# One layer of a hybrid encoder: the last stage's gate weights load through the norm's scratch, and the embeddings' product gets buffers of its own

## The chip, the cores and the metric

The kernel runs on one core of a Trainium2 chip. The metric is the device time of one execution in microseconds (us). The kernel before took 1815.24 us as the median of three runs (1814.98, 1815.24 and 1816.43).

The engines are named as in the profile: PE is TensorE (matrix products; PEld is its weight load), DVE is VectorE, ACT is ScalarE, POOL is GpSimd. SP is the engine whose queue issues nearly all transfers (DMA) of this kernel. Each engine works through its own instructions strictly in the order in which they stand.

## The reference, cut to what matters

The layer handles 1024 prompt tokens and 64 sample tokens of width 1024. The change touches the last two steps of `_layer`, the down projection of the FFN and the per-layer embeddings:

```
    f = (jax.nn.silu(f @ W['w_ffn_gate']) * (f @ W['w_ffn_up'])) @ W['w_ffn_down']
    x = x + _rmsnorm(f, W['norm_ffn_post'])
    gate = jax.nn.sigmoid(_rmsnorm(x, W['norm_ple_pre']) @ W['w_ple_gate'])
    pe = gate * (p @ W['w_ple_proj'])
    x = x + _rmsnorm(pe, W['norm_ple_post'])
```

`w_ffn_down` is 2816 x 1024, `w_ple_gate` is 1024 x 1024. Everything is float32.

## The kernel before

A float32 product is built from two halves: every operand is split into a high part (ACT copies it to the matrix engine's rounded format) and a low part (DVE subtracts), and each product is three matmuls, high by high, high by low and low by high (`split`, lines 124 to 126; `mm3`, line 128). Weights are thus always loaded, split, and then used.

**The down projection** (`ffn_down`) is done in seven block products (i = 0 to 6, the tuple that starts at line 1326), each of 11 steps (p = 0 to 10). A step loads 512 KB: a block of activations from the scratch `sd` and a block of weights from `td` or from `w_ffn_down` itself (`load`, line 1275). ACT and DVE split them, and PE runs 12 matmuls of 512 columns, or 14 in products that also handle the sample tokens against the tile `as` (line 1341). The raw loads rotate through four buffers: two of the tag `wraw` of the pool W, and two `raw` of the pool "ffn2". The split halves rotate through three pairs: two `wh`/`wl` (tags `whi`, `wlo` of W) and one `dh`/`dl`.

**The last stage** works on nine tiles of tokens in the order 4, 5, 6, 7, 0, 8, 1, 2, 3 (`TOKS`). `ple_first` takes a tile's FFN result, normalizes it, adds the residual (`post`), normalizes again, transposes on PE and splits the result into `hT` (`pre`). `ple_second` multiplies `hT` by the split gate weights, takes the sigmoid, multiplies by `q` (the product p @ w_ple_proj, computed at the start of the kernel and kept in the scratch `qd`), normalizes, adds and stores. The first two `ple_first` run inside product 6.

**The gate weights** are eight slabs of 128 x 1024 (512 KB each). `ple_weight` loads one slab, ACT copies its high half into the big tile `H` (free by then), POOL subtracts for the low half. In the kernel before, the slab lies in a `wraw` buffer (`slab`, line 953), and `ple_weight` is called in steps 0 to 8 of product 4: call 0 loads three norm gains, calls 1 to 8 one slab each. `q` lies in a `whi` buffer.

**What sets the order.** The program is recorded in the order of the code; a scheduler then places each engine's instructions by its own estimate of when their inputs and buffers are ready, so a load can stand well ahead of its place in the code. A tile's buffer is reused only after its last reader is done; the waits follow from that.

Of the kernel before, what the change touches and what calls it, by code (L numbers as in the profile page):

```python
# [8 lines left out]
F32 = mybir.dt.float32  # L9
F32R = mybir.dt.float32r  # L10
# [6 lines left out]
D = 1024  # L17
# [51 lines left out]
class Net:  # L69
# [1191 lines left out]
    def ffn_down(self, PA, P):  # L1261

        nc, W = self.nc, self.W
        V, A = nc.vector, nc.scalar
        acc = self.acc = [PA.pool.tile([128, D], F32, name=f"acc{t}") for t in range(9)]
        AS = P.pool.tile([128, 22, 2 * DEC], F32R, name="as")
        sample = self.ad.rearrange("(k p) t -> p k t", p=128)

        def rows(k0, k1):
            s = P.tile([128, 2, 512], F32, "raw", "raw").rearrange("p a b -> p (a b)")[:, :(k1 - k0) * DEC].rearrange("p (k t) -> p k t", t=DEC)  # L1270
            nc.sync.dma_start(s, sample[:, k0:k1])
            self.split(AS[:, k0:k1, :DEC], AS[:, k0:k1, DEC:], s)
        ni = [0]

        def load(i, q, p):

            n = ni[0] = ni[0] + 1
            raw = W.tile([128, 8, 128], F32, name="raw", tag="wraw", bufs=2).rearrange(
                "p (a c) b -> p a (c b)", a=2) if n % 2 else P.tile([128, 2, 512], F32, "raw", "raw")
            nc.sync.dma_start(raw[:, 0], self.sd[p, i])  # L1280
            if isinstance(q, int):
                nc.sync.dma_start(raw[:, 1], self.td[p, q])
            else:
                r = (2 * p + q[0]) * 128
                nc.sync.dma_start(raw[:, 1], self.I["w_ffn_down"][0, r:r + 128, q[1] * 512:q[1] * 512 + 512])
            if n % 3:
                h, l = (W.tile([128, 8, 128], F32R, name=x, tag=t, bufs=2).rearrange("p (a c) b -> p a (c b)", a=2)
                        for x, t in (("wh", "whi"), ("wl", "wlo")))
            else:
                h, l = (P.tile([128, 2, 512], F32R, x, x) for x in ("dh", "dl"))  # L1290
            self.split(h, l, raw)
            return h, l
        lo, hi = slice(0, 512), slice(512, 1024)

        def c11(i, x):
            V.tensor_add(acc[i][:, lo], acc[i][:, lo], x)

        def c21(i, x):
            V.tensor_add(acc[4 + i][:, lo], acc[4 + i][:, lo], x)

        def c22(i, x):
            V.tensor_add(acc[4 + i][:, hi], acc[4 + i][:, hi], x)

        def copy(d, s):
            def f(i, x):
                A.activation(acc[d + i][:, s], x, AF.Copy)
            return f

        def q1(x):
            A.activation(acc[8][:, lo], x, AF.Copy)  # L1310

        def q2(x):
            A.activation(acc[8][:, hi], x, AF.Copy)
            V.tensor_add(acc[8][:, lo], acc[8][:, lo], x)

        def q3(x):
            V.tensor_add(acc[8][:, hi], acc[8][:, hi], x)
        B = {}

        def bank(n):  # L1320
            return self.ps.tile([128, 512], F32, name="z", tag=(XB + ZB)[n])
        self.ps.alias = {}
        rows(0, 16)
        first = []

        for i, q, b, new, end, sq in ((0, (1, 0), 4, True, copy(0, lo), (2, 1, True, q1)),
                                      (1, (0, 0), 0, True, c11, (4, 0, True, q2)),
                                      (2, 3, 0, False, copy(4, lo), None),
                                      (3, 1, 4, True, copy(4, hi), None),
                                      (4, 2, 4, False, c21, None),  # L1330
                                      (5, 0, 0, False, c22, (4, 0, True, None)),
                                      (6, (1, 1), 0, False, copy(0, hi), (4, 1, False, q3))):
            for p in range(11):
                h, l = load(i, q, p)
                if not i and p == 7:
                    rows(16, 22)
                if sq:
                    if sq[2] and not p:
                        Q = bank(sq[0])
                    for j, x in enumerate((h, l)):  # L1340
                        nc.tensor.matmul(Q, AS[:, 2 * p + sq[1]], x[:, 1], start=sq[2] and p == j == 0, stop=p == 10 and j == 1,
                                         skip_group_check=not sq[2])
                    if p == 10 and sq[3]:
                        sq[3](Q)
                for n in range(4):
                    if new and not p:
                        B[b + n] = bank(b + n)
                    c = slice(n * 128, n * 128 + 128)
                    for j, (x, y) in enumerate(((h, h), (h, l), (l, h))):
                        nc.tensor.matmul(B[b + n], x[:, 0, c], y[:, 1], start=new and p == j == 0, stop=p == 10 and j == 2,  # L1350
                                         skip_group_check=not new)
                    if p == 10:
                        end(n, B[b + n])
                if i == 4 and p < 9:
                    self.ple_weight(PA, p)
                if i == 6 and p in (5, 8):
                    self.ps.alias = PAL
                    first.append(self.ple_first(PA, None, len(first)))
        return first

    def ple_weight(self, PA, i):

        nc = self.nc
        if not i:
            self.pw = []
            self.gb = [self.bcast(PA, n) for n in ("norm_ffn_post", "norm_ple_pre", "norm_ple_post")]
            return
        k = i - 1
        raw = self.slab(self.I["w_ple_gate"][0, k * 128:(k + 1) * 128])
        h, l = (self.H[:, k, i, 0:D] for i in range(2))  # L1370
        nc.scalar.activation(h, raw, AF.Copy)
        nc.gpsimd.tensor_sub(l, raw, h)
        self.pw.append((h, l))

    def ple_first(self, PA, P, i):

        nc = self.nc
        gf, gp, _ = self.gb
        t = TOKS[i]
        r, c0 = 128 if t < 8 else DEC, t * 128  # L1380
        x = self.acc[t]
        xr = PA.tile([128, D], F32, "xr", "xr")[:r]
        nc.sync.dma_start(xr, self.x2[c0:c0 + r])
        xs = PA.tile([128, D], F32, "xn", "xn")[:r]
        if t == 8:
            self.low_rows(x[:r], x, xs)
            x = x[:r]
        self.post(PA, [x[:, :512], x[:, 512:]], gf, xr, x, xs)
        PT = P if i % 3 == 2 else PA
        h = PT.tile([128, 8, 256], F32R, "hT", f"hT{i % 3}")  # L1390
        self.pre(PA, x, gp, h[:, :, 0:r], h[:, :, r:2 * r])
        q = self.W.tile([128, 8, 128], F32R, name="wh", tag="whi", bufs=2).bitcast(F32).rearrange("p a b -> p (a b)")[:r]
        nc.sync.dma_start(q, self.qd[c0:c0 + r])
        return x, h, q

    def ple_second(self, P, i, x, h, q):
        nc = self.nc
        U = self.pw
        t = TOKS[i]
        r = x.shape[0]  # L1400
        pe = self.W.tile([128, 8, 128], F32, name="raw", tag="wraw", bufs=2).rearrange("p a b -> p (a b)")[:r]
        xs = P.tile([128, D], F32, "xq", "xq")[:r]
        last = i == 8
        cuts = [slice(a, b) for a, b in (((0, 512), (512, 768), (768, 1024)) if last else ((0, 512), (512, 1024)))]
        for s in cuts:
# [48 lines left out]
def body(tc, I, O, dbg=None, upto=99):  # L1454
    with ExitStack() as ctx:
        N = Net(ctx, tc, I, O, dbg, upto)
        nc = tc.nc
# [80 lines left out]
        with pool("wout", "right") as PW:  # L1538
            N.HS = PW.tile([128, 8, 2 * DEC], F32R, name="HS")
            with pools(tc, "mrgB", dict(braw=1, ga=2, gs=2)) as P:  # L1540
                raw = mA[0].tile([128, TOK], F32, "braw", "braw")
# [10 lines left out]
        PA = ctx.enter_context(pools(tc, "acc", dict(ss=4, xr=1, xn=2, hT0=1, hT1=1)))  # L1552
        with pools(tc, "ffn2", dict(raw=2, dh=1, dl=1), "right") as P:
            A = N.ffn_down(PA, P)
        with pools(tc, "ple", dict(ss=4, hT2=1, xq=1)) as P:
            for t in range(2, 9 + PD):
                if t < 9:
                    A.append(N.ple_first(PA, P, t))
                if t >= PD:
                    N.ple_second(P, t - PD, *A[t - PD])  # L1560
# [27 lines left out]
```

## Time and profile before

| | |
|---|---|
| three runs | 1814.98, 1815.24, 1816.43 us |
| the profiled execution | 1819.19 us, its span 1817.40 us |
| granted TensorE clock, mean over the span | 0.97 of full speed |
| PE / DVE / ACT / POOL busy | 1704.4 / 1040.1 / 728.3 / 524.9 us |
| transfers | 249.83 MB, 137 GB/s mean |
| the down projection's matmuls (line 1350) | 1445.5 to about 1718.5 us of the span |
| the gate weights' eight loads are issued | 1573.7 to 1618.0 us |

The span is the stretch from the first to the last instruction that the trace records; the execution's own time is 1.79 us longer. All durations in this document come from the profiled execution, whose time lies 3.95 us above the runs' median. In rows of a timeline, the first two numbers are start and duration in us; at the end, in square brackets, stands how long the engine was idle before, and what released it.

### The profile page before, as it was taken

How to read it: one execution, taken by the hardware profiler on the slowest of the kernel's cores; microseconds unless marked ns; L12 is line 12 of the kernel's file. 1: busy time of each engine (PE TensorE's matmuls, PEld its weight loads, DVE VectorE, ACT ScalarE, POOL GpSimd, SP SyncE). 2: the span in 40 equal slices, each digit the busy share in tenths (PEclk: the TensorE clock that was granted, in tenths of full speed). 3: DMA queues.
4: the chain of work that ended last, by engine and by line, in shares of the span. 5: the costliest groups of instructions: out<-in, count | busy, mean ns of one | idle time of the engine just before them, and what ended most of it. 6: DMA issues, size and time to landing. Idle time of an engine off the chain costs nothing.

```text
span 1817.4 us, 24624 instructions
## 1 busy us (share of the span) xinstructions
PE 1704.4 (94%) x9092; PEld 1486.6 (82%) x9092; DVE 1040.1 (57%) x1589; ACT 728.3 (40%) x1349; POOL 524.9 (29%) x454
## 2 busy tenths in 40 slices
PE   8999897999999889999999499999999999979998
PEld 6999897988898878798887388888888888858786
DVE  7438725426767777855443865555555444445465
ACT  6431124125555555633322433333333333443443
POOL 2026000012323232233331654444444200031264
PEclk9999898999999998899999799999999999999999
DMA  8352544684443432157333154444444475665232
GB/s 285 96 137 61 119 99 133 219 223 109 103 106 98 94 101 82 45 182 233 124 102 102 42 174 153 146 140 141 147 142 129 142 252 174 196 197 188 91 104 87
DMA packets 209704, 249.83 MB, mean 137 GB/s; under 512 B 25376, under 2 KB 159632, under 8 KB 209568
## 3 DMA queue, kind: packets, MB, share of 16 engines
q1 hardware_dynamic: 208928, 246.81, 45.0%
q0 software_dynamic: 656, 1.44, 0.6%
q8 instruction: 72, 1.18, 0.3%
q14 instruction: 48, 0.39, 0.1%
HBM read 161.13 MB, written 72.32 MB: 128 GB/s over the span
## 4 chain that ended last, share of the span: by engine, by line
PE 74%; DVE 12%; DMA 5%; ACT 3%; issue 2%; POOL 1%; SPq 1%; DVEq 0%; POOLq 0%; ACTq 0%
PE pj L1184 13%; PE tr L1184 7%; PE pj L137 6%; PE pj L139 6%; PE pj L138 6%; PE pj L1350 3%; PE z L1350 3%; DVE p L730 3%; PE z L1184 3%; PE av L806 2%; PE z L138 2%; PE z L139 2%; PE z L137 2%; PE av L1350 2%; PE tr L1350 2%
## 5 line engine op out<-in xcount | busy, mean ns | idle before, releaser
L137 PE MATMUL pj<-H,wh 128*128 128x362 f32 (+3 forms) x648 | 218.0, 337 | 6.1 <-DVE ql L629 3.4
L139 PE MATMUL pj<-H,wl 128*128 128x362 f32 (+3 forms) x648 | 215.2, 333 | 0.6 <-DVE wl L115 0.6
L138 PE MATMUL pj<-H,wh 128*128 128x362 f32 (+3 forms) x648 | 214.8, 332 | 0.0
L126 DVE TENSOR_TENSOR wl<-raw,wh 128x1024 fp32r<-128x1024 f32 x96 | 129.6, 1352 | 122.5 <-ACT wh L125 122.2
L732 POOL TENSOR_TENSOR w<-w,p 128x383 f32<-128x383 f32 (+4 forms) x68 | 92.6, 1371 | 315.3 <-DVE w L734 187.2
L125 ACT ACTIVATE wh<-raw 128x1024 fp32r<-128x1024 f32 x96 | 101.1, 1057 | 124.5 <-PE z L1350 55.9
L137 PEld LDWEIGHTS pj<-H,wh 128*128 128x128 f32 x648 | 123.0, 190 | 7.8 <-DVE ql L629 3.6
L139 PEld LDWEIGHTS pj<-H,wl 128*128 128x128 f32 x648 | 122.7, 189 | 1.5 <-DVE wl L115 0.8
L138 PEld LDWEIGHTS pj<-H,wh 128*128 128x128 f32 x648 | 122.9, 190 | 1.0 <-issue 0.4
L1184 PE MATMUL pj<-H,s 128*128 128x512 f32 x480 | 118.2, 395 | 0.0
L1184 PEld LDWEIGHTS pj<-H,s 128*128 128x128 f32 x480 | 89.8, 188 | 20.8 <-DVE c L1219 0.3
L125 ACT ACTIVATE s<-st 128x512 fp32r<-128x512 f32 x80 | 50.1, 628 | 125.3 <-PE pj L1184 110.9
L126 DVE TENSOR_TENSOR s<-st,s 128x512 fp32r<-128x512 f32 x80 | 66.0, 827 | 46.9 <-ACT s L125 46.0
L148 POOL TENSOR_TENSOR rs<-rs,mhalf 128x1 f32<-128x1 f32 (+1 forms) x54 | 34.7, 644 | 181.8 <-DVE rs L147 181.5
L119 ACT ACTIVATE wh<-raw 128x1024 fp32r<-128x1024 f32 (+1 forms) x52 | 46.6, 898 | 94.8 <-PE av L138 46.3
L781 DVE TENSOR_TENSOR wtl<-tr,wth 128x512 fp32r<-128x512 f32 (+2 forms) x112 | 55.3, 496 | 50.7 <-ACT wth L780 50.3
L780 ACT ACTIVATE wth<-tr 128x512 fp32r<-128x512 f32 (+2 forms) x112 | 50.3, 453 | 84.6 <-PE tr L776 43.9
L115 DVE TENSOR_TENSOR wl<-raw,wh 128x1024 fp32r<-128x1024 f32 (+1 forms) x50 | 51.1, 1021 | 56.5 <-ACT wh L119 56.5
L1120 POOL TENSOR_TENSOR st<-raw 128x512 f32<-128x512 f32 x40 | 57.6, 1442 | 75.9 <-DVE s L126 41.5
L1184 PE MATMUL tr<-T,s 128*128 128x512 f32 x240 | 62.3, 399 | 17.1 <-ACT s L125 17.1
L728 ACT ACTIVATE p<-z 128x512 f32<-128x512 f32 (+4 forms) x116 | 59.0, 509 | 42.7 <-PE z L830 16.7
L730 DVE TENSOR_TENSOR_SCAN p<-p,zero 128x384 f32<-128x384 f32 (+4 forms) x68 | 73.9, 1094 | 0.2
(558 smaller groups left out, 4672.1 us busy)
## 6 DMA issues: line engine op xcount, KB each, us to landing
sd<-c SPq DMA_DIRECT2D x77, 256.0 KB, 2.7
raw<-sd SPq DMA_DIRECT2D x77, 256.0 KB, 2.8
raw<-in_w_in_dram SPq DMA_DIRECT2D x32, 512.0 KB, 5.4
raw<-in_w_ffn_gate_dram SPq DMA_DIRECT2D x22, 512.0 KB, 3.8
raw<-in_w_ffn_up_dram SPq DMA_DIRECT2D x22, 512.0 KB, 4.7
wd<-in_w_ffn_down_dram SPq DMA_DIRECT2D x44, 256.0 KB, 3.5
td<-wd SPq DMA_DIRECT2D x22, 512.0 KB, 3.2
raw<-td SPq DMA_DIRECT2D x44, 256.0 KB, 3.1
```

The source lines that it names most:

```text
L125: self.nc.scalar.activation(wh, raw, AF.Copy)
L126: self.nc.vector.tensor_sub(wl, raw, wh)
L137: self.nc.tensor.matmul(out, wh, xh, start=i == 0, stop=False)
L138: self.nc.tensor.matmul(out, wh, xl, start=False, stop=False)
L139: self.nc.tensor.matmul(out, wl, xh, start=False, stop=i == n - 1)
L728: nc.scalar.activation(p, z, AF.Sigmoid, scale=-1.0)
L730: nc.vector.tensor_tensor_scan(p[:, ::-1], p[:, ::-1], self.zero.to_broadcast([128, n]), 1.0 if carry is None else carry, op0=OP.mult, op1 ...
L732: (nc.gpsimd if e == 'g' else nc.vector).tensor_tensor(w[:, :n - 1], w[:, :n - 1], p[:, 1:], op=OP.mult)
L781: nc.vector.tensor_sub(wl[:, a:b], ps[:, a:b], wh[:, a:b])
L1120: op(t, x, y)
L1184: self.nc.tensor.matmul(out, a[i][:, k], b[j][:, k], start=start and k == i == j == 0, stop=stop and k == 3 and i == 1, skip_group_check=n ...
L1350: nc.tensor.matmul(B[b + n], x[:, 0, c], y[:, 1], start=new and p == j == 0, stop=p == 10 and j == 2, skip_group_check=not new)
```

## The change

`ple_weight` is called at other places, loads into another buffer, and `q` moves to buffers of its own:

```diff
-                if i == 4 and p < 9:
-                    self.ple_weight(PA, p)
+                if (i, p) == (1, 0) or 2 <= i <= 5 and p in (3, 8):
+                    self.ple_weight(PA, 0 if i == 1 else 2 * i - 3 + (p == 8))
...
-        raw = self.slab(self.I["w_ple_gate"][0, k * 128:(k + 1) * 128])
         h, l = (self.H[:, k, i, 0:D] for i in range(2))
+        raw = PA.tile([128, D], F32, "xn", "xn")
+        nc.sync.dma_start(raw, self.I["w_ple_gate"][0, k * 128:(k + 1) * 128])
         nc.scalar.activation(h, raw, AF.Copy)
         nc.gpsimd.tensor_sub(l, raw, h)
...
-        q = self.W.tile([128, 8, 128], F32R, name="wh", tag="whi", bufs=2).bitcast(F32).rearrange("p a b -> p (a b)")[:r]
-        nc.sync.dma_start(q, self.qd[c0:c0 + r])
-        return x, h, q
-
-    def ple_second(self, P, i, x, h, q):
+        return x, h
+
+    def ple_second(self, P, i, x, h):
...
+        q = P.tile([128, D], F32, "q", "q")[:r]
+        nc.sync.dma_start(q, self.qd[t * 128:t * 128 + r])
...
-        with pools(tc, "ple", dict(ss=4, hT2=1, xq=1)) as P:
+        with pools(tc, "ple", dict(ss=4, hT2=1, xq=1, q=2)) as P:
```

So the code has two slabs in each of the products 2 to 5, the slabs lie in the two `xn` buffers (the scratch of the norms, unused until `ple_first`), and `q` is loaded in `ple_second`. In the built program the two `q` buffers begin at bytes 205248 and 209344 of each partition; `as`, the sample tokens of the down projection, lies at 201696 to 212960, so `q` can be loaded only after the last matmul that reads `as`. `xq`, at 201152, lies over `as` before and after.

The scheduler does not keep the slabs where the code has them. SP's queue in product 0, where the norm gains (`gb_...`) are loaded; `ad` holds the sample tokens, `xr` a residual, `sd` and `in_w_ffn_down` a step's operands. Before:

```order
L950 DMA gb_norm_ple_pre<-in_norm_ple_pre_dram 128x1024
L950 DMA gb_norm_ple_post<-in_norm_ple_post_dram 128x1024
L1383 DMA xr<-x_8619 128x1024
L1271 DMA raw<-ad 128x6x64
L1280 DMA raw<-sd 128x512
L1285 DMA raw<-in_w_ffn_down_dram 128x512
```

The same place of SP's queue now:

```order
L950 DMA gb_norm_ple_pre<-in_norm_ple_pre_dram 128x1024
L950 DMA gb_norm_ple_post<-in_norm_ple_post_dram 128x1024
L1371 DMA xn<-in_w_ple_gate_dram 128x1024 x2
L1271 DMA raw<-ad 128x6x64
L1384 DMA xr<-x_8619 128x1024
L1280 DMA raw<-sd 128x512
L1285 DMA raw<-in_w_ffn_down_dram 128x512
```

Two slabs stand ahead of `ad` and of the operands of product 0's steps 10 and 9, which follow in this order, before as now. The third and fourth slab stand four steps' operands further on, the others singly; all eight stand ahead of product 2's first load.

ACT in products 0 and 1, as the difference (`H` is written by the slabs' copies, `wh` and `dh` by the splits of the steps, `as` by that of the sample tokens):

```order
 L125 ACTIVATE dh<-raw 128x1024
 L125 ACTIVATE wh<-raw 128x1024 x2
-L125 ACTIVATE dh<-raw 128x1024
+L1372 ACTIVATE H<-xn 128x1024
+L125 ACTIVATE dh<-raw 128x1024
+L1372 ACTIVATE H<-xn 128x1024
 L125 ACTIVATE as<-raw 128x6x64
 L125 ACTIVATE wh<-raw 128x1024 x2
 L125 ACTIVATE dh<-raw 128x1024
-L125 ACTIVATE wh<-raw 128x1024
+L1372 ACTIVATE H<-xn 128x1024
+L125 ACTIVATE wh<-raw 128x1024
```

The copies of the slabs now stand between the splits of product 0's last steps and product 1's first ones; the eighth stands behind the split of product 1's step 6, and product 4 has none.

ACT at the end of product 6 (`L1306` copies its four sums out, `L1414` is the sigmoid, `xn` and `xq` are norms, `acc_13218` to `acc_13221` the tiles 4 to 7 and `acc_13214` tile 0). Before:

```order
L982 ACTIVATE xn,ss<-acc_13221 128x512 x2
L1414 ACT_TABLE_LOAD
L1414 ACTIVATE raw<-z 128x512
L1010 ACTIVATE xn,ss<-acc_13221 128x1024
L982 ACTIVATE xn,ss<-acc_13214 128x512
L1414 ACTIVATE raw<-z 128x512
L125 ACTIVATE wh<-raw 128x1024 x2
L125 ACTIVATE hT<-tr 128x4x128 x2
L982 ACTIVATE xq,ss<-raw 128x512 x2
L1306 ACTIVATE acc_13214<-pj 128x512
```

The same place now:

```order
L125 ACTIVATE wh<-raw 128x1024 x2
L1010 ACTIVATE xn,ss<-acc_13220 128x1024
L125 ACTIVATE hT<-tr 128x4x128 x2
L982 ACTIVATE xn,ss<-acc_13221 128x512 x2
L1306 ACTIVATE acc_13214<-pj 128x512
L1306 ACTIVATE acc_13215<-pj 128x512
L1306 ACTIVATE acc_13216<-av 128x512
L1306 ACTIVATE acc_13217<-z 128x512
L1010 ACTIVATE xn,ss<-acc_13221 128x1024
```

The last two splits of product 6 stood behind both sigmoids of the first `ple_second`; now they stand ahead of all of them, and the first sigmoid comes after the sums are copied out.

## Rows read from the trace of the kernel before

**Rows 1.** The page's first part: busy us, share of the span, instructions.

```profile
PE 1704.4 (94%) x9092; PEld 1486.6 (82%) x9092; DVE 1040.1 (57%) x1589; ACT 728.3 (40%) x1349; POOL 524.9 (29%) x454
```

**Rows 2.** Table by stretch: length, busy us per engine (instructions), granted clock, DMA share, GB/s.

```profile
core 0: us, PE busy (x) PEld busy (x) DVE busy (x) ACT busy (x) POOL busy (x), PEclk, DMA share, GB/s
1445.00:1490.00 45.00, 45.00 (x197) 36.49 (x196) 23.24 (x24) 18.08 (x21) 0.00 (x0) 1.00 0.80 263
1490.00:1522.00 32.00, 32.00 (x142) 26.23 (x141) 12.95 (x12) 11.08 (x11) 0.00 (x0) 1.00 0.52 165
1522.00:1590.00 68.00, 68.00 (x300) 55.81 (x299) 31.56 (x27) 30.86 (x34) 2.88 (x2) 1.00 0.61 192
1590.00:1630.00 40.00, 28.78 (x108) 21.61 (x107) 15.00 (x9) 15.60 (x16) 17.54 (x7) 0.91 0.63 204
...
1700.00:1720.00 20.00, 16.35 (x68) 12.28 (x66) 6.97 (x10) 8.56 (x17) 1.36 (x3) 0.91 0.10 29
1720.00:1800.00 80.00, 80.00 (x366) 64.50 (x366) 52.67 (x74) 35.92 (x84) 43.23 (x28) 1.00 0.32 108
```

**Rows 3.** Timeline, products 4 and 5: PE's longest waits.

```profile
1593.05 0.51 PE L1350 MATMUL z<-dl,dh 128*128 128x512 f32 x1 [1.40 <-DVE dl L126]
...
1607.35 0.89 PE L1350 MATMUL z<-dh 128*128 128x512 f32 x2 [4.60 <-ACT dh L125]
...
1618.41 1.22 PE L1350 MATMUL z<-wh 128*128 128x512 f32 x2 [3.69 <-ACT wh L125]
```

**Rows 4.** Chain that ended last, 1580 to 1630 us, in order of time.

```profile
1582.65 5.71 DMA raw<-in_w_ple_gate_dram
...
1589.52 2.41 POOL H L1372
...
1592.32 3.13 DMA raw<-td
...
1595.55 1.07 ACT wh L125
```

**Rows 5.** Timeline of the end of product 6: PE's two waits, ACT, DVE.

```profile
1708.77 0.50 PE L1341 MATMUL z<-wh,as 128*128 128x512 f32 x1 [2.50 <-ACT wh L125]
...
1715.09 0.50 PE L1341 MATMUL z<-wh,as 128*128 128x512 f32 x1 [1.15 <-ACT wh L125]
```

```profile
1707.66 1.06 ACT L125 ACTIVATE wh<-raw 128x1024 fp32r<-128x1024 f32 x1 [0.76 <-DVE raw L1415]
```

```profile
1706.94 0.69 DVE L1415 TENSOR_TENSOR raw<-raw,wh 128x512 f32<-128x512 f32 x1 [3.29 <-ACT raw L1414]
```

**Rows 6.** SP's queue in product 0: issue and its length.

```profile
1462.63 0.79 SPq L1383 DMA_DIRECT2D xr<-x  x1
...
1470.34 0.42 SPq L1285 DMA_DIRECT2D raw<-in_w_ffn_down_dram  x1
```

**Rows 7.** Table by stretch, ten us of product 0.

```profile
1460.00:1470.00 10.00, 10.00 (x46) 8.21 (x45) 4.01 (x4) 3.18 (x3) 0.00 (x0) 1.00 0.89 318
```

**Rows 8.** Timeline, product 0's step 9: ACT's split, DVE's, and PE's use of each.

```profile
1475.35 1.06 ACT L125 ACTIVATE wh<-raw 128x1024 fp32r<-128x1024 f32 x1 [2.33 <-DMA raw<-in_w_ffn_down_dram]
```

```profile
1476.44 1.23 DVE L126 TENSOR_TENSOR wl<-raw,wh 128x1024 fp32r<-128x1024 f32 x1 [2.83 <-ACT wh L125]
```

```profile
1480.20 0.40 PE L1341 MATMUL av<-wh,as 128*128 128x512 f32 x1
...
1481.36 0.39 PE L1341 MATMUL av<-wl,as 128*128 128x512 f32 x1
```

**Rows 9.** Timeline: DVE's subtraction without and with POOL's beside it.

```profile
1586.32 1.22 DVE L126 TENSOR_TENSOR wl<-raw,wh 128x1024 fp32r<-128x1024 f32 x1 [3.46 <-ACT wh L125]
...
1590.42 2.58 DVE L126 TENSOR_TENSOR dl<-raw,dh 128x1024 fp32r<-128x1024 f32 x1 [2.87 <-ACT dh L125]
```

**Rows 10.** DMA issues: KB each, median us to landing; 1440 to 1520, then all.

```profile
xr<-x SPq DMA_DIRECT2D x1, 512.0 KB, 9.1
```

```profile
raw<-in_w_ple_gate_dram SPq DMA_DIRECT2D x8, 512.0 KB, 4.1
wh<-qd SPq DMA_DIRECT2D x8, 512.0 KB, 3.5
```

**Rows 11.** Waits, 1570 to 1640: us in total, times, longest.

```profile
ACT H L1371 <- DMA raw<-in_w_ple_gate_dram: 14.9, 8, 3.2
```

## The prediction, made before the changed kernel was run

> **What bounds the kernel now.** I began with the page's busy times: PE is busy for 94% of the span [rows 1], so the kernel gets faster where PE stops waiting, and nowhere else. The second view was the table by stretch over the part that the change can reach, the down projection and the last stage [rows 2]. The reader is to look for stretches whose PE time is shorter than the stretch. There are two. From 1590 to 1630 PE is busy 28.78 of 40 us, and its granted clock is 0.91, so part of what it does runs at 1.2 in place of 2.4 GHz. From 1700 to 1720 it is busy 16.35 of 20 us, again at 0.91. In the four other stretches shown PE has no gap and the full clock.
>
> The third view was the timeline of the first gap, for what PE waits on: splits of its own steps, by ACT or DVE, the longest 4.60 and 3.69 us [rows 3]. The chain of waits says why these are late [rows 4]: a slab of gate weights takes 5.71 us to land, POOL subtracts for 2.41 us, and only then is the step's operand loaded (3.13 us) and split (1.07 us). The slab lies in one of the four raw buffers through which the steps' operands run, so each slab takes that buffer out of the rotation until POOL is done. The timeline of the second gap [rows 5] shows ACT's split of product 6's step 9 released by DVE's product with `q`, which reads a `wh` buffer; PE then waits 2.50 and 1.15 us for the two last splits.
>
> **The change part by part.**
>
> *The slabs leave the raw buffers and product 4.* What goes is the first gap. Its idle time is 40 - 28.78 = 11.2 us, and the lost clock (1 - 0.91) x 40 = 3.6 us, together 14.8 [rows 2]. Counted another way: the stretch before it runs 300 matmuls in 68 us, so 40 us should hold 176; there are 108, and the 68 missing at 0.227 us are 15.5. I take 15.0. The low end is 11.2, if the clock did not come back with the idle time; the high end 15.5. Products 4 and 5 would then look like the stretch from 1522 on, which has the same operands and no gap. No other wait stands right behind the one removed: the splits there are released by PE itself.
>
> *The slabs arrive in products 0 and 1.* The same eight loads (512 KB), eight ACT copies of 1.06 us and eight POOL subtractions of 2.4 us are done there, and this is where the change must pay. The cover is that PE's operands are split ahead of use. In product 0's step 9, the tightest that I found, ACT ends at 1476.41 and PE needs the result at 1480.20; DVE ends at 1477.67 and PE needs that at 1481.36 [rows 8]. The slack is 3.8 and 3.7 us. Against it stand:
> - the transfers. From 1460 to 1470 the DMA engines are 0.89 busy and move 318 GB/s [rows 7]. SP's queue is in order and already backed up: the residual issued at 1462.63 lands after 9.1 us [rows 6, 10], and step 9's weights, issued at 1470.34, are what ACT waits for until 1475.35 [rows 6, 8]. Two slabs ahead of them add 2 x 0.524 MB / 318 GB/s = 3.3 us.
> - ACT's copies, which wait for their slab in order, with the splits queued behind them. Of the two copies of 1.06 us, most lies in the 2.33 us in which ACT is idle anyway before that split [rows 8]. I count nothing for these.
> - POOL's subtraction beside DVE's: 2.58 against 1.22 us, 1.36 more [rows 9].
>
> The sum at step 9 is 3.3 + 1.4 - 3.7 = 1.0 us of waiting. The next pair of slabs goes out about 15 us later, at the start of product 1, with the backlog draining (the DMA share falls to 0.52 from 1490 on, rows 2); I put 0.5 us on it and nothing on the four that follow singly. So 1.5 us. The low end is 0. The high end: both pairs at 3.3 + 2.1 + 2.4 (two copies and a whole subtraction in the way) - 3.7 = 4.1 us each, and behind each the clock cost that the second gap shows, (1 - 0.91) x 20 = 1.8 us [rows 2]: 12 us. I take the value near the low end, because the rows that set it are measured in that very stretch.
>
> The Trainium skill, "SBUF — State Buffer", section "Who interferes with whom", speaks against this move: VectorE and GpSimd share a port pair as an exclusive lock, so that one of them waits for the other's whole instruction. This trace agrees: the subtraction of 2.58 us began inside one of POOL's. By that rule a DVE split could lose up to a whole POOL instruction, 2.4 us, in place of my 1.36, and the wait at step 9 would be 2.0 us in place of 1.0.
>
> *`q` leaves the `whi` buffers.* What goes is the second gap: 20 - 16.35 = 3.65 us idle and 0.09 x 20 = 1.8 us of clock, 5.4 together [rows 2]. The last two splits of product 6 no longer wait for the first tile's sigmoid and product, and stand ahead of them on ACT. PE loses nothing by having its filler (the first tile's gate products) moved behind: all of that work remains and is ready, and with tiles 4 to 6 transposed it is 3 x 48 matmuls at 0.227 us, 33 us, while ACT copies the sums out. What is late next is `q` of the first tile, which must wait for the last read of `as` and then 3.5 us for its landing [rows 10]. DVE needs it after the first half of the first gate product and its sigmoid, which is 24 matmuls or 5.4 us after the down projection's end; so it arrives earlier than it is needed. The low end is 0, if a new wait takes the place of the old one; the high end 5.4. I take 5.4, as the 80 us behind it run without a wait at POOL 43 and DVE 53 us busy [rows 2], and there PE has more work, not less, to cover the others.
>
> The rest (the residual's load behind `ad`, the gains' call in product 1, which the scheduler leaves where it was) moves nothing that PE waits for: 0.
>
> Sum: -15.0 - 5.4 + 1.5 = -18.9 us. Against the profiled execution that is 1819.19 - 18.9 = 1800.3, and against the median of the runs, 3.95 us lower, 1815.24 - 18.9 = 1796.3. I predict on the median's basis.
>
> **The rivals.**
> 1. *The slabs stall products 0 and 1 in earnest.* For it: the DMA share of 0.80 there against 0.63 where they are now [rows 2], and landings of 9.1 us against 4.1 [rows 10]. Against: the slack of 3.7 us, and that slabs no longer hold up the steps' own buffers. At the high end of the cost, 12 us: 1815.24 - 20.4 + 12 = 1806.8; from 5 us on 1799.8. Time 1800 to 1807.
> 2. *The second gap comes back.* `q`'s buffers lie over `as`; were DVE, in order, to stop at the first product with `q`, the splits of the next tile's transposes would queue behind it and PE would run dry. Against: 3.5 us to land against 5.4. The 5.4 us are lost: 1801.7.
> 3. *Slower.* The copies of the slabs hold ACT for every slab, as now: eight slabs cost 15.0 us now, 1.9 each, of which ACT's waits for their landing are 14.9 in all [rows 11]. Where a landing takes 9.1 in place of 4.1 us, and the splits stand behind the copies in order, each slab would cost about twice that, 3.8 us: 30 us in products 0 and 1 against 20.4 gained, 1824.8. It decides for slower from (20.4 + 3.6) / 8 = 3.0 us per slab. Against: it needs slack near zero at every slab, and after 1490 the DMA engines are half idle.
>
> That the slabs are not spread as the code has them, two to a product, is no rival: the order shows it, and the sum is made for where they stand.
>
> **How the numbers follow.** The forecast has 0.77, with 1793 to 1800 as its own range (0 to 4 us of cost, 1 us for the spread of the runs and the sum's first term); rival 1 has 0.11, rival 2 0.08, rival 3 0.04. The predicted time is 1796.3. The range from 1792.5 to 1806 takes in the forecast, rival 2 and most of rival 1; it leaves out rival 3 and the worst of rival 1. A change of 0.2%, 3.6 us, is about what can be told from none here. Faster: all of the forecast and rival 2, and rival 1 but for a rest, 0.93. The same: a rival 1 worse than I bounded it, 0.03. Slower: 0.04.
>
> **What would show it right or wrong.** In the table by stretch, products 4 and 5 with PE busy throughout at clock 1.00. In product 0, PE's wait at step 9 near 1 us, and none over 2 us up to product 2; if several of 3 us stand there, with ACT's copies of the slabs ahead of them, rival 1 or 3 holds. At the end of product 6, no idle PE before the last two steps; a wait of DVE on `q` with PE idle behind it means rival 2. The prediction would be wrong, too, if the gap in products 4 and 5 stayed without any slab in it: then the raw buffers were not its cause.

## The result, and the profile after

The changed kernel takes 1793.57 us (median of 4 runs, 1792.61 to 1796.34) beside 1815.11 us of the kernel before on the same chip (1810.88 to 1816.43): ratio 0.9888, 95% interval 0.9868 to 0.9907. The forecast was 1796.3.

The profiled execution took 1793.02 us, its span 1791.2. That is 26.2 us less span than before, but not all of it is the change's. The first matmul `tr<-wh,wl` of product 0 starts at 1450.30 us before and at 1443.67 now; what runs up to there is not touched by the change. The timelines of PE, before and after:

```profile
1450.30 0.40 PE L1350 MATMUL tr<-wh,wl 128*128 128x512 f32 x1
```

```profile
1443.67 0.40 PE L1350 MATMUL tr<-wh,wl 128*128 128x512 f32 x1
```

So I compare from this matmul to the end of the span ("from product 0 on"): 1817.4 - 1450.3 = 367.1 us before, 1791.2 - 1443.7 = 347.5 after, a gain of 19.6. The table by stretch, cut at equal distances from that matmul: 78 us (products 0 and 1 and the start of 2), 122 us (most of products 2 to 5), 80 us (product 6 and the first tiles), the rest. Columns as in [rows 2]. Before:

```profile
1450.30:1528.30 78.00, 78.00 (x341) 63.66 (x340) 37.11 (x37) 28.98 (x32) 0.00 (x0) 1.00 0.67 221
1528.30:1650.30 122.00, 110.78 (x467) 89.10 (x466) 55.10 (x43) 52.97 (x57) 20.43 (x8) 0.97 0.62 199
1650.30:1730.30 80.00, 76.35 (x339) 61.50 (x338) 39.32 (x55) 34.76 (x61) 21.62 (x17) 0.98 0.37 120
```

After:

```profile
1443.70:1521.70 78.00, 76.43 (x329) 61.04 (x328) 48.41 (x37) 35.44 (x39) 21.14 (x8) 1.00 0.80 269
1521.70:1643.70 122.00, 122.00 (x538) 100.70 (x537) 55.73 (x49) 50.65 (x56) 0.00 (x0) 1.00 0.58 186
1643.70:1723.70 80.00, 80.00 (x372) 65.35 (x371) 55.46 (x76) 44.16 (x88) 37.48 (x27) 1.00 0.38 129
```

Read the number of PE's matmuls in each. In the middle stretch it rises from 467 to 538: 71 more at 122 / 538 = 0.227 us are 16.1 us gained, and the stretch is full. So are the 80 us behind it, in which product 6 ends (its last matmul starts at 1680.26 now). In the first it falls from 341 to 329, 12 x 0.227 = 2.7 us lost: POOL, idle there before, now has its eight subtractions. What is left of the 19.6, 6.2 us, came behind product 5.

Two waits of PE stand in products 0 and 1, both for a low half by DVE, in the second and sixth step of product 1 (p = 1 and p = 5). Here they are, the first with the rows on either side:

```profile
1482.36 0.63 PE L1350 MATMUL pj<-wh 128*128 128x512 f32 x2
1483.91 0.50 PE L1341 MATMUL z<-wl,as 128*128 128x512 f32 x1 [0.92 <-DVE wl L126]
1484.24 0.39 PE L1350 MATMUL pj<-wl,wh 128*128 128x512 f32 x1
...
1498.90 0.50 PE L1341 MATMUL z<-wl,as 128*128 128x512 f32 x1 [0.56 <-DVE wl L126]
```

Undisturbed, a matmul starts every 0.227 us and its row lasts 0.39, so the idle time in brackets is less than the delay. From 1482.36 to 1484.24 three starts take 1.88 us in place of 0.68: the first wait costs 1.2 us. The second costs 0.8 by the same count. Three more delays, too short to be listed as waits, cost 0.8 together; each stands behind a low half that DVE made beside POOL. The sum is 2.8 us, the loss that the matmuls show.

The timelines of DVE, POOL and ACT (of the changed kernel) ahead of the first wait show what delays it:

```profile
1481.26 2.59 DVE L126 TENSOR_TENSOR wl<-raw,wh 128x1024 fp32r<-128x1024 f32 x1 [2.78 <-DMA raw<-in_w_ffn_down_dram]
```

```profile
1480.36 5.75 POOL L1373 TENSOR_TENSOR H<-xn,H 128x1024 fp32r<-128x1024 f32 x2 [8.44 <-ACT H L1372]
```

```profile
1479.22 1.06 ACT L1372 ACTIVATE H<-xn 128x1024 fp32r<-128x1024 f32 x1 [2.00 <-DMA xn<-in_w_ple_gate_dram]
1480.18 1.04 ACT L125 ACTIVATE wh<-raw 128x1024 fp32r<-128x1024 f32 x1
```

ACT waits 2.00 us for the slab, with the step's split behind it. Then POOL starts on the slab 0.9 us before DVE starts on the step, and DVE takes 2.59 in place of 1.22 us [rows 9]. So two things make the low half late: ACT's split comes late, and DVE's subtraction takes longer.

`q` arrives early: its first load is issued at 1677.92 and lands 3.3 us later (median of 8), and DVE's first product with it is at 1687.8.

### The profile page after: what moved, and what is told of

The parts are those of the page before. It is cut to its first block, busy times and chain, and to the rows that moved or that the text cites. A ratio compares the mean times of both kernels' runs of the same rounds, so it can differ in the third digit from the quotient of the medians.

```text
span 1791.2 us, 24621 instructions
## 1 busy us (share of the span) xinstructions
PE 1688.2 (94%) x9092; PEld 1474.8 (82%) x9092; DVE 1049.7 (59%) x1589; ACT 728.4 (41%) x1349; POOL 527.2 (29%) x454
## 4 chain that ended last, share of the span: by engine, by line
PE 73%; DVE 13%; DMA 6%; ACT 3%; issue 3%; SPq 1%; POOL 1%; DVEq 0%; POOLq 0%; ACTq 0%
PE pj L1184 14%; PE tr L1184 8%; PE pj L137 6%; PE pj L139 6%; PE pj L138 6%; DVE p L730 3%; PE z L1350 3%; PE z L1184 3%; PE pj L1350 3%; PE tr L1350 2%; PE z L138 2%; PE z L137 2%; PE z L139 2%; PE av L806 2%; PE tr L776 1%
## 5 line engine op out<-in xcount | busy, mean ns | idle before, releaser
L126 DVE TENSOR_TENSOR wl<-raw,wh 128x1024 fp32r<-128x1024 f32 x96 | 135.7, 1416 | 105.4 <-ACT wh L125 102.4
```

The source lines that it names most:

```text
L126: self.nc.vector.tensor_sub(wl, raw, wh)
```

## The experiments

"From product 0 on" is taken from each kernel's profile, "idle" is the sum of PE's own waits of over 0.15 us in it. Times are medians beside those of the kernel before on the same chip: 1815.11 for the changed kernel, 1814.50 for `q_only`, `weights_only`, `place_only` and `held4`, 1815.57 for `held`, `buffer_only`, `every2` and `q_late`, 1813.25 for `held_early`, `changed_again` and `dve_low`.

| kernel | us | ratio, 95% | from product 0 on | idle |
|---|---|---|---|---|
| before | 1815.11 | | 367.1 | 14.83 |
| `q_only` | 1810.12 | 0.9974 [0.9963, 0.9986] | 361.0 | 10.13 |
| `weights_only` | 1803.26 | 0.9933 [0.9917, 0.9949] | 352.3 | 5.36 |
| `every2` (one run) | 1800.89 | | 353.5 | 4.55 |
| `place_only` | 1797.84 | 0.9902 [0.9885, 0.9919] | 348.6 | 1.42 |
| `held4` | 1797.12 | 0.9903 [0.9886, 0.9920] | 348.6 | 1.62 |
| `held` | 1798.89 | 0.9897 [0.9880, 0.9915] | 349.4 | 2.54 |
| `held_early` | 1794.60 | 0.9903 [0.9887, 0.9920] | 347.7 | 2.24 |
| changed | 1793.57 | 0.9888 [0.9868, 0.9907] | 347.5 | 1.48 |
| `changed_again` | 1795.29 | 0.9897 [0.9883, 0.9912] | 347.4 | 1.45 |
| `buffer_only` | 1798.81 | 0.9905 [0.9886, 0.9923] | 349.8 | 2.49 |
| `q_late` | 1795.85 | 0.9890 [0.9875, 0.9905] | 347.7 | 1.61 |
| `dve_low` | 1793.64 | 0.9888 [0.9873, 0.9903] | 344.8 | 0 |

All diffs are against the changed kernel and shortened at `...`.

**`q_only`**: the gate weights as before.

```diff
-                if (i, p) == (1, 0) or 2 <= i <= 5 and p in (3, 8):
-                    self.ple_weight(PA, 0 if i == 1 else 2 * i - 3 + (p == 8))
+                if i == 4 and p < 9:
+                    self.ple_weight(PA, p)
...
-        raw = PA.tile([128, D], F32, "xn", "xn")
-        nc.sync.dma_start(raw, self.I["w_ple_gate"][0, k * 128:(k + 1) * 128])
+        raw = self.slab(self.I["w_ple_gate"][0, k * 128:(k + 1) * 128])
```

> The gate weights go through the wraw buffers in product 4, as before; only q has its own buffers and is asked for in ple_second. Theory (q, asked for before the last splits, took their wh buffers): the gap at the end of product 6 goes, 5.4 us by the idle time and the clock of rows 2, so 1809.7 us beside 1815.1; in the trace no wait of PE for the splits of product 6's last two steps, while the gap in products 4 and 5 stays, with PE idle 11 us in 40. Rival (the gap in products 4 and 5 leaves the operands late to the end, so that the second gap hangs on the first): the second gap stays and the time is 1815.

Measured: -6.1 us from product 0 on. PE's longest waits are still in products 4 and 5, and none is left behind them:

```profile
1523.70:1645.70 122.00, 111.76 (x467) 89.91 (x466) 55.20 (x43) 53.13 (x57) 19.93 (x8) 0.96 0.61 199
1645.70:1725.70 80.00, 80.00 (x370) 65.77 (x369) 50.79 (x68) 43.51 (x79) 29.29 (x21) 1.00 0.40 131
```

The second gap is `q`'s and doesn't hang on the first.

**`weights_only`**: `q` as before.

```diff
+        q = self.W.tile([128, 8, 128], F32R, name="wh", tag="whi", bufs=2).bitcast(F32).rearrange("p a b -> p (a b)")[:r]
+        nc.sync.dma_start(q, self.qd[c0:c0 + r])
-        return x, h
+        return x, h, q
...
-        q = P.tile([128, D], F32, "q", "q")[:r]
-        nc.sync.dma_start(q, self.qd[t * 128:t * 128 + r])
...
```

> The gate weights go through xn as in the changed kernel; q is asked for in ple_first and lies in a wh buffer, as before. Theory (two independent causes): the gap in products 4 and 5 goes and 1.6 us of waits come in products 0 and 1, the end of product 6 keeps its waits of 2.50 and 1.15 us: -15.0 + 1.6 = -13.4, 1801.7 us beside 1815.1; q alone and weights alone add up to the whole, -21.5, within 3 us. Rival (the second gap hangs on the first): already as fast as the changed kernel, 1793.6.

Measured: -14.8 us from product 0 on. The end of product 6 has its old waits of [rows 5], to the hundredth:

```profile
1694.32 0.50 PE L1341 MATMUL z<-wh,as 128*128 128x512 f32 x1 [2.50 <-ACT wh L125]
1699.06 0.50 PE L1341 MATMUL z<-wh,as 128*128 128x512 f32 x1 [1.15 <-ACT wh L125]
```

By the profiles the parts add up: -6.1 - 14.8 = -20.9 against -19.6 together. By the times they don't within the 3 us that I had allowed: 4.4 and 11.2 us, 15.6 in all, against 21.5 (18.0 in `changed_again` below); the intervals of these ratios are 4 to 7 us wide. What the profiles show is that each gap stays when the other is gone, so neither hangs on the other.

**`place_only`**: the spread calls, but through `wraw`.

```diff
-        raw = PA.tile([128, D], F32, "xn", "xn")
-        nc.sync.dma_start(raw, self.I["w_ple_gate"][0, k * 128:(k + 1) * 128])
+        raw = self.slab(self.I["w_ple_gate"][0, k * 128:(k + 1) * 128])
```

> As the changed kernel, q included, but the gate weights are loaded into the wraw buffers, two to a product in products 2 to 5. Theory (a slab takes one of the four raw buffers out of the steps' rotation until POOL is done, some 8 us from issue to release by rows 4, so the step that takes that buffer next is late): the gap is spread, not gone: some of the eight slabs cost PE a wait of 1 to 2 us each, since a product's other steps can win back part between them; 1798 to 1806 us. Rival (eight slabs in ten steps were too close together for SP's queue, ACT and POOL; the buffer doesn't matter): no waits in products 2 to 5, at most the 1793.6 us of the changed kernel, or 1792 as products 0 and 1 have no slabs.

**`held4`**: `xn`, at the old place: the calls as in `q_only`, and each load behind the step's.

```diff
...
-        nc.sync.dma_start(raw, self.I["w_ple_gate"][0, k * 128:(k + 1) * 128])
+        with self.tc.issue_after(self.ld.ins):
+            nc.sync.dma_start(raw, self.I["w_ple_gate"][0, k * 128:(k + 1) * 128])
```

> As the changed kernel, q included, and the gate weights in xn, but each of their loads is held behind a load of a step of product 4, so that they run in products 4 and 5, where they ran before. Theory (the raw buffers): the same loads, copies and subtractions at the old place cost nothing or little, since the steps' raw buffers stay in rotation: 1792 to 1795 us, no wait of PE over 1 us from 1590 to 1630. Rival (their traffic, copies on ACT and POOL's subtraction beside DVE's, is the cost): the gap of 11 us comes back with the clock's 3.6, 1807 us.

These two cross place and buffer. `held4` has the old traffic at the old place, and most of the gap is gone: 1.62 us of idle PE in place of 10.13 in `q_only`, which differs in the buffer and in that no load is held there. The loads of `held4` are not further apart: the eight are issued within 30.5 us, in `q_only` within 43.7. Of the 71 matmuls that the gap cost the middle stretch, 54 are back (521 against 467). So the buffer was most of the cost; the 17 still missing, 3.9 us, are what the copies, POOL's work and the transfers can have cost at most, and the time, 1797.12, lies 2 us above what I had expected. But `place_only` has the old buffers, and most of the gap is gone there too (1.42 us idle, 16 matmuls missing, 1797.84): my expectation of 1 to 2 us for each of several slabs failed. The middle stretch of `place_only`, then of `held4`:

```profile
1523.50:1645.50 122.00, 120.46 (x522) 97.23 (x521) 62.34 (x48) 55.14 (x61) 16.84 (x7) 1.00 0.65 215
```

```profile
1526.00:1648.00 122.00, 120.38 (x521) 98.57 (x520) 64.61 (x48) 57.15 (x62) 20.25 (x8) 0.99 0.66 216
```

A slab in a raw buffer costs much only where the next follows soon. How soon was the next question.

**`every2`**: through `wraw`, one slab in every second step from product 4 on.

```diff
-                if (i, p) == (1, 0) or 2 <= i <= 5 and p in (3, 8):
-                    self.ple_weight(PA, 0 if i == 1 else 2 * i - 3 + (p == 8))
+                s = i * 11 + p - 44
+                if (i, p) == (1, 0) or 0 <= s < 16 and s % 2 == 0:
+                    self.ple_weight(PA, 0 if i == 1 else s // 2 + 1)
...
+        raw = self.slab(self.I["w_ple_gate"][0, k * 128:(k + 1) * 128])
```

> As the changed kernel, q included, but the gate weights go through wraw, one in every second step from product 4 on (before: one in every step; the spread one: two in eleven). Theory (a slab holds one of the four raw buffers for a time, and how much of it PE sees depends on how many steps the rotation has to recover before the next slab): the gap between the two, 4 to 10 us of idle PE in products 4 and 5, so 352 to 358 us from product 0 on where the spread one takes 348.6 and slabs in every step 361.0. Rival (only slabs in successive steps hurt, as two of them then follow each other in one of the two wraw buffers with a single step between): 348.6 +- 0.5.

Measured: 353.5 us, 4.55 idle, inside the theory's range. With `wraw` and `q` alike, slabs in every step, in every second, and two in eleven leave 10.13, 4.55 and 1.42 us of idle PE. SP's queue and POOL show the hold: a slab's load goes out at 1586.74, POOL ends with it at 1591.41 + 2.39 = 1593.80, and at 1593.83 the next slab's load goes out:

```profile
1586.74 0.33 SPq L956 DMA_DIRECT2D raw<-in_w_ple_gate_dram  x1
1593.83 0.33 SPq L956 DMA_DIRECT2D raw<-in_w_ple_gate_dram  x1
```

```profile
1591.41 2.39 POOL L1373 TENSOR_TENSOR H<-raw,H 128x1024 fp32r<-128x1024 f32 x1 [4.69 <-ACT H L1372]
```

This slab holds its buffer for 7.1 us, and from the third slab on each load goes out within 0.03 us of POOL's end on the one before. In `place_only` the loads are 12.7 to 17.8 us apart.

**`buffer_only`**: the calls as in `q_only`, the rest as changed. On all five engines the instructions stand in the same order as in the changed kernel.

> As the changed kernel, but the gate weights are asked for where the kernel before asks, in product 4, one in each of the first nine steps. The instructions stand in the same order on every engine as in the changed kernel, since their loads move up to where xn is free either way. Theory: the place in the code does nothing once the buffer is xn; 1793.6 us, the part from product 0 on 347.5 +- 0.5. Rival (something else than the order differs, as addresses or semaphores): a difference of over 1 us.

Measured: 1798.81 us, with a ratio whose interval overlaps that of the changed kernel; 349.8 us in its profile, 2.3 more, although the order is the same. By its own sign the expectation failed. One of its two waits was 1.87 us, and in four us right behind it the granted clock was 0.57 and 11 matmuls ran, where 17 or 18 run at full clock, 1.5 us lost:

```profile
1510.00:1514.00 4.00, 4.00 (x11) 3.15 (x11) 2.02 (x2) 0.00 (x0) 0.00 (x0) 0.57 0.62 189
```

The same order took 347.4 and 347.7 us in `changed_again` and `q_late`, so I take the 2.3 us for what two profiles of one order can differ by, which the later comparisons have to allow for; that addresses or semaphores differ is not ruled out by one profile. The place that the code names did not change the order; the buffer decided where the slabs run.

**`q_late`**: `q` in a `wh` buffer, asked for in `ple_second`.

```diff
-        q = P.tile([128, D], F32, "q", "q")[:r]
+        q = self.W.tile([128, 8, 128], F32R, name="wh", tag="whi", bufs=2).bitcast(F32).rearrange("p a b -> p (a b)")[:r]
         nc.sync.dma_start(q, self.qd[t * 128:t * 128 + r])
...
```

> As the changed kernel, but q lies in a wh buffer, as before; it is asked for in ple_second, as in the changed kernel. The instructions stand in the same order on every engine. Theory (what cost PE was that q was asked for ahead of the last two steps' splits, not which buffer it has; asked for behind them it takes a wh buffer that nobody needs): no waits at the end of product 6, the part from product 0 on 347.5 +- 0.5, 1793.6 us. Rival (its own buffers matter, since a wh buffer is given back only when the down projection's last matmul has read it, later than DVE needs q): 1 to 5.4 us slower.

Measured: 1795.85 us, 347.7. `q`'s own buffers were not needed: `weights_only` has the same `wh` buffer and loads `q` in `ple_first`, and takes 352.3. What counted was asking for it behind the last steps' splits.

**`held`** and **`held_early`**: `xn`, and each load held as in `held4`, at the places that the code names (steps 3 and 8 of products 2 to 5), or at steps 0 and 5.

> As the changed kernel, and each load of gate weights held behind the load of the step at which the code calls it, so that they run two to a product in products 2 to 5, in xn. Theory (in products 0 and 1 the backlog of transfers and the subtraction beside POOL's cost 1.6 us; from product 2 on there is slack for one slab at a time): no wait of PE over 0.3 us from product 0 to the end of product 6; the part from product 0's first product of the weights to the end, 347.5 us in the changed kernel, takes 346, and the time is 1792. Rival (wherever a slab's split meets the steps' own it costs about the same, as with the spread slabs in wraw and the held ones in product 4, 1.7 and 1.6 us): 347.5, 1793.5.

> As held, but the gate weights' loads are held behind steps 0 and 5 of products 2 to 5 in place of 3 and 8. Theory (the 2.54 us of the held one came from one slab whose copy stood on ACT ahead of the copies of a product's sums and waited for its landing; moved away from a product's end it finds slack): no wait of PE over 0.3 us in the down projection, 346.0 +- 0.4 us from product 0 on, 1.5 to 3.8 us less than the runs of the changed kernel's order (347.5 and 349.8), as a time about 1792 to 1796. Rival (a slab's copy that waits for its landing on ACT in order costs 1.5 to 2.5 us wherever it is): 347.5 to 349.

Both theories failed: no wait in products 0 and 1, but others elsewhere, 2.54 and 2.24 us. In `held`, ACT stands for 2.57 us before a slab that hasn't landed, with the copies of product 3's sums behind it, and PE waits for these banks. ACT's timeline, and PE's:

```profile
1577.37 1.06 ACT L125 ACTIVATE wh<-raw 128x1024 fp32r<-128x1024 f32 x1 [1.66 <-PE tr L1350]
1581.00 1.06 ACT L1373 ACTIVATE H<-xn 128x1024 fp32r<-128x1024 f32 x1 [2.57 <-DMA xn<-in_w_ple_gate_dram]
1581.96 1.07 ACT L1306 ACTIVATE acc<-z 128x512 f32<-128x512 f32 x2
```

```profile
1582.60 0.50 PE L1350 MATMUL z<-dh 128*128 128x512 f32 x1 [2.54 <-ACT acc L1306]
```

`held_early` avoids that one, and PE waits 0.90 and 1.34 us for low halves by DVE, each time 2.6 us long beside a subtraction on POOL. Its 347.7 us lie in the rival's range, but not by the rival's cause. Here are DVE and POOL at the first:

```profile
1524.11 2.59 DVE L126 TENSOR_TENSOR wl<-raw,wh 128x1024 fp32r<-128x1024 f32 x1 [4.11 <-ACT wh L125]
```

```profile
1523.21 2.42 POOL L1374 TENSOR_TENSOR H<-xn,H 128x1024 fp32r<-128x1024 f32 x1 [14.08 <-ACT H L1373]
```

POOL ends at 1525.63, DVE at 1526.70, 1.07 us later. In `held_early` and in `place_only` each of the eight slabs brings such a pair with it, in `held` five do: ACT copies the slab and then splits the step it had held up, so that POOL begins about one ACT copy before DVE.

**`changed_again`** and **`dve_low`**: the changed kernel once more, and the low halves of the gate weights on DVE.

```diff
-        nc.gpsimd.tensor_sub(l, raw, h)
+        nc.vector.tensor_sub(l, raw, h)
```

> The changed kernel once more, beside held_early on the same chip. Expected by both theories: 1793 to 1799 us; PE waits 1.5 to 2.6 us in all in products 0 and 1, each time for a low half by DVE, 347.5 to 350 us from product 0 on.

> As the changed kernel, but the low halves of the gate weights are subtracted on DVE in place of POOL. Theory (the waits of 0.5 to 1.9 us in products 0 and 1 come from DVE's subtractions of a step beside POOL's, 2.6 to 3.0 in place of 1.2 us): POOL idle there, every subtraction 1.2 us, no wait of PE for a low half over 0.3 us, 346.0 to 346.5 us from product 0 on. Rival (the waits come from transfers that land late or from ACT): the waits of 1.5 us or more stay, and eight more subtractions on DVE make them no shorter.

Measured: with `dve_low` PE has no wait from product 0 to the last stage: 344.8 us, 2.6 less than `changed_again` and below the 346.0 to 346.5 expected. The grouped rows of DVE and POOL over 1440 to 1525 us, of the changed kernel:

```profile
L126 DVE TENSOR_TENSOR wl<-raw,wh 128x1024 fp32r<-128x1024 f32 x17 | 27.3, 1618 | 20.9 <-ACT wh L125 17.9 <-DMA raw<-in_w_ffn_down_dram 2.8
...
L1373 POOL TENSOR_TENSOR H<-xn,H 128x1024 fp32r<-128x1024 f32 x8 | 21.1, 2652 | 60.3 <-ACT H L1372 60.3
```

and of `dve_low`, with the first stretch of its table:

```profile
L126 DVE TENSOR_TENSOR wl<-raw,wh 128x1024 fp32r<-128x1024 f32 x17 | 20.7, 1223 | 20.5 <-ACT wh L125 20.5
L1373 DVE TENSOR_TENSOR H<-xn,H 128x1024 fp32r<-128x1024 f32 x8 | 9.8, 1222 | 5.5 <-ACT H L1372 5.4
```

```profile
1446.20:1524.20 78.00, 78.00 (x341) 63.58 (x340) 46.03 (x45) 36.26 (x40) 0.00 (x0) 1.00 0.80 274
```

The slabs still run in products 0 and 1, with the DMA share as high (0.80 in both), and PE is back at the 341 matmuls of before; the five kernels that have POOL's subtractions there show 319 to 330. But not only POOL is out: the scheduler places the slabs' loads anew, the third of them two steps' operands further ahead, and product 1's second step is split 33.5 us behind product 0's first `tr<-wh,wl`, in the changed kernel 36.5. The timeline of `dve_low` at product 0's step 9, DVE and PE:

```profile
1475.95 1.22 DVE L126 TENSOR_TENSOR wl<-raw,wh 128x1024 fp32r<-128x1024 f32 x1 [3.37 <-ACT wh L125]
```

```profile
1477.23 0.50 PE L1341 MATMUL av<-wl,as 128*128 128x512 f32 x1
```

The low half is ready at 1475.95 + 1.22 = 1477.17, and PE takes it at 1477.23. Of the 3.7 us of slack [rows 8] less than 0.1 is left. So late transfers alone came just short of a wait, and `dve_low` by itself doesn't part them from POOL. The changed kernel does, at its first wait. The kernel before at the same step, DVE's subtraction and the first uses of the high and of the low half by PE:

```profile
1484.73 1.23 DVE L126 TENSOR_TENSOR wl<-raw,wh 128x1024 fp32r<-128x1024 f32 x1 [2.01 <-ACT wh L125]
```

```profile
1488.45 0.40 PE L1341 MATMUL z<-wh,as 128*128 128x512 f32 x1
...
1490.76 0.40 PE L1341 MATMUL z<-wl,as 128*128 128x512 f32 x1
```

Counted from product 0's first `tr<-wh,wl`, DVE is done at 1485.96 - 1450.30 = 35.7 us before and at 1483.85 - 1443.67 = 40.2 in the changed kernel, 4.5 later: 3.2 by ACT's later split, the rest by the longer subtraction. The slack was 1490.76 - 1485.96 = 4.8 us. But PE's order there has changed, too: before, it comes to the low half 2.3 us after the high one, now three matmuls, 0.7 us, after it. That leaves 3.2 us of slack, 3.5 with the 0.3 that PE is late by then. By this count neither the late split nor the pair alone would have made PE wait; together they make 4.5 us, and it waits. The times can't tell the two kernels apart (1793.64 and 1795.29 us on one chip, overlapping intervals); the 2.6 us are read from the profiles alone, one of each.

## Why the prediction was right, and where it was not

**The slabs leave the raw buffers: -15.0 predicted, -16.1 measured** by matmuls in the middle stretch. `held4` against `q_only` shows the buffer as the cause of 54 of the 71 matmuls, 12.3 us. The prediction left out that the cost per slab is no constant: `every2` and `place_only` show that it grows as the slabs follow closer, and that spreading them in the old buffers would have won nearly as much. Rival 3's price of 1.9 us a slab rested on that constant too.

**The slabs arrive in products 0 and 1: +1.5 predicted, +2.7 measured** (12 matmuls). The terms were real, the step and the size were not. The prediction put 1.0 us on product 0's step 9, out of 3.3 us of transfers, 1.4 of POOL beside DVE and a slack of 3.7, and 0.5 on the second pair. The profile after has no wait at step 9, since the two costs did not meet there. It is the first of these two subtractions of DVE, 1.2 us each:

```profile
1472.29 2.36 DVE L126 TENSOR_TENSOR wl<-raw,wh 128x1024 fp32r<-128x1024 f32 x2
```

They met in product 1's second step, at the second pair of slabs: 3.2 us of a later split and 1.4 of DVE, against a slack that PE's changed order had cut from 4.8 to 3.2. The prediction left that order out. It had nothing on the slabs that follow singly, and the wait of 0.56 us in the sixth step stands beside two of them. That the transfers alone reach no wait is luck: in `dve_low` they left less than 0.1 us.

**Of DVE and POOL**, the rows show the delay whole: DVE's instruction that begins inside one of POOL's ends 1.1 us after POOL's end, near its own 1.22 us. From product 0 on this happens, in the traces of all these kernels together, to 78 subtractions of 128x1024 on DVE, wherever in POOL's instruction they begin, and each ends 1.08 or 1.09 us after it. The Trainium skill, "SBUF — State Buffer", section "Who interferes with whom", says just that: the one that comes second waits for the other's instruction. The price that it gave for step 9, 2.0 in place of 1.0 us, is borne out by no wait at that step, but the mechanism is; the repeats show single waits from 0.3 to 1.9 us.

**`q`: -5.4 predicted, -6.1 measured alone**, and 347.5 - 352.3 = -4.8 on top of the weights. Rightly told, but credited to the wrong half of the edit: `q_late` gains the same without the new buffers.

**Sum: -18.9 predicted, -19.6 measured** from product 0 on; 1796.3 us against 1793.57, and against 1795.29 and 1798.81 in the repeats of the same order. That the sum is nearer than its terms is luck: 1.1 us too little gain in the middle stretch and 1.2 too little cost ahead of it cancel, and what is left is `q`'s term.

**The rivals.** Rival 1 (5 us and more in products 0 and 1) fails by the 2.7 us, rival 2 by the 80 us behind the middle stretch, in which PE is busy throughout, and by `q`, which waits landed for DVE. Rival 3 had one right part: ACT held before a slab's landing costs PE something, as `held` shows with 2.54 us, but once in eight slabs; in the changed kernel ACT waits 2.00 us for a slab ahead of the split that comes late.

## What to carry over

A load that passes through a pipeline's own buffers should be priced by how long it holds one (issue, landing, copy, last reader) against the distance to the next such load: close together they starve the pipeline, far apart they cost little, and other buffers or a wider spacing will do. Where a scheduler moves loads up to the first free buffer, the buffer sets the place, not the line that asks. Before giving GpSimd a subtraction for relief, see whether VectorE has one of its own in the same microsecond. And a slack read from the old order holds only as long as the order does: a test that moves an operation to another engine can move loads as well.

## What had not been expected of the hardware

The same two waits, 2.50 and 1.15 us, stood at the end of product 6 in the kernel before and in `weights_only`, with PE busy for the same 16.35 of 20 us. In the first the granted clock was 0.91 [rows 2] and 68 matmuls ran, in the second it was 1.00 and 73 ran. `weights_only`:

```profile
1690.00:1710.00 20.00, 16.35 (x73) 12.37 (x72) 9.07 (x14) 8.66 (x17) 3.45 (x3) 1.00 0.14 53
```

So the 1.8 us of clock that I had added to this gap does not follow from the wait alone: it came in one execution and stayed out in another. Nor does the length of a wait tell: `held4` has a granted clock of 0.57 from 1583 to 1587 behind waits of 0.70 and 0.92 us, `buffer_only` the same behind one of 1.87, and `weights_only` 1.00 behind one of 2.50. The part ahead of the change differs between profiles as well: in the profiles of all these kernels product 0 starts between 1443.7 and 1450.3 us, which is why spans say less here than the time from product 0 on.
